# TensorE's order written out by hand in three attention stages

## The chip, the cores and the metric
The kernel runs on one core of a Trainium2 chip. The time is the device time of one launch in microseconds (us), the median of 3 runs. TensorE (PE) multiplies matrices and transposes, VectorE (DVE) and ScalarE (ACT) work on whole tiles, GpSimd (POOL) does a few copies, SyncE's queue (SP) starts the transfers from memory.

## What is computed
Two layers of a first block and one of a second, on 512 tokens of width 1024 in 32-bit floats. All three have an attention of 8 heads of width 64, and other projections of the same input beside it. Cut to this:

```
# first block, twice (l = 0, 1)
u = rmsnorm(x, norm_mix[l]);  proj = u @ w_in[l]
q, k, v, iq, ik, iw, cB, cC, ch, g = split(proj)          # q, k with rotary positions
s = q @ k.T / 8, kept where an index score is among the largest
y_attn = (softmax(s) @ v) @ w_attn_out[l]
gates = sigmoid(g)                                        # 2 x 1024 columns
x = x + (gates0 * y_attn + gates1 * y_conv) @ w_mix_out[l];  x = x + mlp(x)
# second block
qa, ka, va, qm, km, vm, og, ig, fg = split(h @ w_in)
attn = dilated attention of qa, ka, va                    # 3 patterns, added by their weights
qm, km = silu(short convolution of qm, km)
hm = chunked mLSTM(qm, km, vm, gates of ig, fg);  y = concat(attn, hm) @ w_out
```

## The kernel before
**Products in three matmuls.** A 32-bit factor is split into a high part, rounded to the type that the matmuls take (fp32r), and the low rest. A product is hi·hi + lo·hi + hi·lo. The weights are split as they come: `split` casts on ScalarE (L222) and subtracts on VectorE (L223), into rings of four buffers. So a cast of a weight unit waits until TensorE is done with the unit four before it.

**Projections.** `linear` makes a list of pieces. A piece is one column tile of 128 with 4 of the 8 blocks of the inner dimension: 4 x 3 = 12 matmuls of 512 columns, on L290, L291 and L292 (in `linear_tok`, used for the values of the mLSTM, L441 to L443, 6 matmuls a piece). The first piece of a weight unit carries a mark at which later units are fetched and split.

**Attention.** The 8 heads go in 4 pairs, the 512 queries in 4 blocks of 128. A unit is one pair and one block (`attn_unit`), 16 in a stage, and has three parts. `scores` (L555): two matmuls for each head, 128, 256, 384 or 512 keys wide (at least 256 on TensorE); VectorE adds the mask and reduces (L558), ScalarE takes the exponential (L563, with its sum), VectorE inverts that (L565), ScalarE scales (L566). `transp` (L574): one transpose for each block of 128 keys and head; the result is copied out of its bank by VectorE (L577) for head 0 and by ScalarE (L579) for head 1. `product`, once for a pair: 40 matmuls (L589) with the values into one bank, then a split on ScalarE and VectorE (L466, L467).
The score matmuls need their operands stacked: high and low part above each other (`two_part`, L605 and L606; `doubled`, L612 to L614, and a copy by GpSimd, L615). `parts` does both heads of a pair.

**Banks.** Four accumulation banks serve the projections (mm), three serve scores and transposes (at), one the products (ot). Within a unit the heads take one at bank each, and the bank goes on to the third tile behind it: head 1 of the transposes of a unit gets the bank that head 0 of the next unit's scores had.

**What sets the order.** `attn_pieces` gives a list: operands, the scores of unit t, the transposes of unit t - 1, and the product of a pair when its last unit is transposed. `interleave` mixes this list with the pieces of projections: the first gate (16 pieces, L894 to L897) in the first block, the convolution's and the mLSTM's projections in the second block (L1387 to L1394), where three functions of the gates, `gates1` to `gates3`, hang on pieces too. This list is not yet the order on an engine. A scheduler takes the list as priority and puts the instructions of each engine in an order by its own estimate of when their operands are there; so transposes, scores and products can be split up and mixed with projection matmuls.

Of the kernel before, what the change touches and what calls it, by code (L numbers as in the profile page):

```python
# [126 lines left out]
def blocks_kernel(ctx: ExitStack, tc: tile.TileContext, a: dict, out: bass.AP, stop=None):  # L127
# [114 lines left out]
    def linear(W, row0, kts, c0, widths, xs, evac, parts_=1, narrow=False, newbank=mmbank, bytile=False, skip=0):  # L242
# [23 lines left out]
        for part in range(parts_):  # L266
            cs = slice(part * TW, (part + 1) * TW)
            for kbase, kt, us in steps:
                for u in us:
# [3 lines left out]
                    for j, w in enumerate(widths):  # L273
# [5 lines left out]
                        def emit(u=u, j=j, o=o, w=w, kb=kbase, kt=kt, cs=slice(skip, T) if skip and w == P else cs):  # L279
                            if kb == 0:  # L280
                                bank[j] = newbank()
                            n = cs.stop - cs.start
                            ps = bank[j][:w, :n]
                            for k in range(kt):
                                hi, lo = xs(kb + k)
                                wh = u["hi"][:, k, o : o + w]
                                wl = u["lo"][:, k, o : o + w]
                                st = kb + k == 0
                                en = kb + k == total - 1
                                pe.matmul(ps, wh, hi[:, cs], start=st, stop=False)  # L290
                                pe.matmul(ps, wh, lo[:, cs], start=False, stop=False)  # L291
                                S["pe"] = pe.matmul(ps, wl, hi[:, cs], start=False, stop=en)  # L292
                            if kb + kt == total:
# [248 lines left out]
    def attn_unit(pair, i, stacks, PT, V, bias, O):  # L542
# [4 lines left out]
        def scores():  # L547
            qs, ks = stacks[pair]
            if i == NT - 1:
                stacks.pop(pair)  # L550
# [67 lines left out]
    def parts(q32, k32):  # L618

        qs, ks = [], []  # L620
        for hh in range(2):
            r = slice(64 * hh, 64 * hh + 64)
            o = slice(64 - 64 * hh, 128 - 64 * hh)
            qs.append(two_part(r, o, q32[r]))
            ks.append(doubled(r, o, k32[r]))
        return qs, ks

    def attn_pieces(q, k, V, bias, O):

        stacks = {}  # L630

        def stack(pair):
            def f():
                stacks[pair] = parts(q.pop(pair), k.pop(pair))
            return ("do", f)
# [4 lines left out]
        pieces = []  # L640
        I.append(stack(0))
        for t in range(n + 2):
            p = []
            if t < n and t % NT == 1 and t // NT < 3:
                p.append(stack(t // NT + 1))
            if t < n:
                p.append(("do", us[t][0]))
            if 1 <= t <= n:
                p.append(("do", us[t - 1][1]))
            if t >= 2 and t % NT == 1:  # L650
                p.append(("do", us[t - 2][2]))
            for it in p:
                pieces.append([it])
        return pieces
# [33 lines left out]
    def layer1(l, nextprep):  # L688
# [205 lines left out]
        for g in range(2):  # L894
            g0p += linear(W, 0, [4, 4], 3396 + 512 * g, [P] * 4, xs, evg0(g))
        at = attn_pieces(q, k, lambda j: V[j], bias, O)
        I.extend(interleave(at, g0p))  # L897
# [265 lines left out]
    def block2():  # L1163
# [223 lines left out]
        pieces = linear(W, 0, [4, 4], 1536, [P] * 4, xs, evconv(qm, 0))  # L1387
        pieces[2] = pieces[2] + [("do", gates1)]
        pieces[6] = pieces[6] + [("do", gates2)]
        pk = linear(W, 0, [4, 4], 2048, [P] * 4, xs, evconv(km, 4))  # L1390
        pk[4] = pk[4] + [("do", gates3)]
        pieces += pk
        pieces += linear_tok(W, 2560, xs, evv(vm))
        I.extend(interleave(attn_pieces(q, k, lambda j: V[j], db, O), pieces))  # L1394
# [384 lines left out]
```

## Time and profile before
| | |
|---|---|
| median of 3 runs | 2046.41 us (2046.17 to 2046.44) |
| the profiled execution | 2044.83 us, its span 2043.0 us |
| mean granted clock of TensorE | 0.997 of full speed |
| PE busy | 2026.1 us, 99% of the span |
| VectorE, ScalarE busy | 76%, 48% |
| stage 1, first score to the first matmul of `w_attn_out` | 223.22 to 299.48 us |
| stage 2, likewise | 921.31 to 997.58 us |
| stage 3, from the first projection of its own | 1486.56 to 1589.43 us |

The span is the time from the first to the last instruction in the trace. A stage is the stretch of one attention. A row of a timeline gives start and duration, the engine, the line and the operation, the tiles written and read, and the number of instructions; in brackets stands how long the engine stood idle before it and what released it. Matmuls are pipelined: the time from one start to the next is what a matmul takes from PE, the duration in the row is longer.

### The profile page before, as it was taken

Reading aid. Unit: us, or ns where it says so; the run is one execution under the profiler, and the core shown is the slowest. Engines: PE = TensorE matmul, PEld = TensorE weight load, DVE = VectorE, ACT = ScalarE, POOL = GpSimd, SP = SyncE. Lnnn points to the kernel's source line nnn. Section 1 sums busy time; section 2 is a strip of 40 time slices with the busy share of each in tenths; the row PEclk is TensorE's granted clock in tenths of the full one; section 3 lists DMA queues with packets and bytes.
Section 4 is the critical chain, followed back from the end, with each engine's and each line's share of the span. In section 5 each row is a group of like instructions: output and inputs, shape, how many; then the busy total and the mean of one; then the engine's idle time right before and its main releaser. Section 6 shows DMA issues by size and latency. Waiting matters only on the chain.

```text
span 2043.0 us, 29780 instructions
## 1 busy us (share of the span) xinstructions
PE 2026.1 (99%) x11632; PEld 1754.7 (86%) x11632; DVE 1547.0 (76%) x2783; ACT 986.6 (48%) x1713; POOL 19.5 (1%) x33
## 2 busy tenths in 40 slices
PE   9999999999999999999999999999999998999999
PEld 7888888899999888888888999999877797999998
DVE  6998667888787659977678888877777386777775
ACT  5323774644444432338655444455377754444442
POOL 0000000000000000000000000000010000000000
PEclk9999999999999999999999999999999999999999
DMA  7233223344444332331224444443221131332321
GB/s 248 83 94 102 73 63 93 100 149 149 150 155 147 105 105 83 100 96 63 73 93 134 145 155 134 155 134 88 87 83 54 50 114 32 104 103 94 114 94 42
DMA packets 203116, 216.62 MB, mean 106 GB/s; under 512 B 10720, under 2 KB 182112, under 8 KB 202976
## 3 DMA queue, kind: packets, MB, share of 16 engines
q1 hardware_dynamic: 202976, 214.73, 33.8%
q8 instruction: 91, 1.49, 0.3%
q14 instruction: 49, 0.40, 0.1%
HBM read 212.60 MB, written 2.10 MB: 105 GB/s over the span
## 4 chain that ended last, share of the span: by engine, by line
PE 95%; DVE 2%; ACT 1%; DMA 0%; issue 0%; SPq 0%; POOL 0%; DVEq 0%; ACTq 0%; POOLq 0%
PE mm L290 14%; PE mm L291 13%; PE mm L292 13%; PE mm L414 7%; PE mm L413 7%; PE mm L412 7%; PE at L290 7%; PE at L291 7%; PE at L292 7%; PE at L555 2%; PE mm L441 1%; PE mm L442 1%; PE mm L443 1%; PE ot L589 1%; PE at L574 1%; PE mm L1583 1%
## 5 line engine op out<-in xcount | busy, mean ns | idle before, releaser
L222 ACT CAST wh<-raw 128x1024 fp32r<-128x1024 f32 (+3 forms) x278 | 283.6, 1023 | 535.0 <-PE mm L413 221.6
L290 PE MATMUL mm<-g,wh 128*128 128x512 f32 (+2 forms) x1360 | 512.6, 378 | 1.7 <-ACT g L1103 1.6
L292 PE MATMUL mm<-g,wl 128*128 128x512 f32 (+2 forms) x1360 | 512.9, 377 | 0.0
L291 PE MATMUL mm<-g,wh 128*128 128x512 f32 (+2 forms) x1360 | 510.4, 375 | 0.0
L223 DVE TENSOR_TENSOR wl<-raw,wh 128x1024 fp32r<-128x1024 f32 (+3 forms) x278 | 329.3, 1186 | 141.3 <-ACT wh L222 140.3
L414 PE MATMUL mm<-g,wl 128*128 128x256 f32 x1288 | 364.6, 283 | 0.0
L413 PE MATMUL mm<-g,wh 128*128 128x256 f32 x1288 | 364.5, 283 | 0.0
L412 PE MATMUL mm<-g,wh 128*128 128x256 f32 x1288 | 363.9, 283 | 0.0
L290 PEld LDWEIGHTS mm<-g,wh 128*128 128x128 f32 x1360 | 255.8, 188 | 49.6 <-issue 4.3
L292 PEld LDWEIGHTS mm<-g,wl 128*128 128x128 f32 x1360 | 256.2, 188 | 45.5 <-issue 1.0
L291 PEld LDWEIGHTS mm<-g,wh 128*128 128x128 f32 x1360 | 256.1, 188 | 44.2 <-DVE g L475 0.3
L412 PEld LDWEIGHTS mm<-g,wh 128*128 128x128 f32 x1288 | 246.8, 192 | 4.7
L413 PEld LDWEIGHTS mm<-g,wh 128*128 128x128 f32 x1288 | 246.8, 192 | 4.6
L414 PEld LDWEIGHTS mm<-g,wl 128*128 128x128 f32 x1288 | 246.8, 192 | 0.2
L290 PE MATMUL at<-g,g 128*128 128x512 f32 x592 | 231.9, 392 | 0.0
L291 PE MATMUL at<-g,g 128*128 128x512 f32 x592 | 231.8, 392 | 0.0
L292 PE MATMUL at<-g,g 128*128 128x512 f32 x592 | 230.6, 389 | 0.1
L222 ACT CAST wh<-ws 128x1024 fp32r<-128x1024 f32 x69 | 72.3, 1048 | 182.3 <-PE mm L413 170.1
L292 PEld LDWEIGHTS at<-g,g 128*128 128x128 f32 x592 | 111.2, 188 | 24.7 <-DVE g L223 0.8
L223 DVE TENSOR_TENSOR wl<-ws,wh 128x1024 fp32r<-128x1024 f32 x69 | 84.5, 1224 | 59.7 <-ACT wh L222 59.7
L290 PEld LDWEIGHTS at<-g,g 128*128 128x128 f32 x592 | 111.7, 189 | 19.9
L291 PEld LDWEIGHTS at<-g,g 128*128 128x128 f32 x592 | 111.7, 189 | 18.6
(272 smaller groups left out, 2685.4 us busy)
## 6 DMA issues: line engine op xcount, KB each, us to landing
raw<-w_in SPq DMA_DIRECT2D x111, 512.0 KB, 3.8
raw<-w_mlp_up SPq DMA_DIRECT2D x64, 512.0 KB, 3.8
raw<-w_mlp_down SPq DMA_DIRECT2D x64, 512.0 KB, 3.6
g<-w_ada SPq DMA_DIRECT2D x96, 256.0 KB, 4.2
raw<-w_gate SPq DMA_DIRECT2D x22, 512.0 KB, 3.7
raw<-w_up SPq DMA_DIRECT2D x22, 512.0 KB, 3.6
raw<-w_down SPq DMA_DIRECT2D x22, 512.0 KB, 3.4
raw<-w_mix_out SPq DMA_DIRECT2D x16, 512.0 KB, 3.7
```

The source lines that it names most:

```text
L222: act.copy(hi, raw)
L223: dve.tensor_sub(lo, raw, hi.bitcast(F32))
L290: pe.matmul(ps, wh, hi[:, cs], start=st, stop=False)
L291: pe.matmul(ps, wh, lo[:, cs], start=False, stop=False)
L292: S["pe"] = pe.matmul(ps, wl, hi[:, cs], start=False, stop=en)
L412: pe.matmul(ps, wh, hi, start=first and m == 0 and k == 0, stop=False, skip_group_check=True)
L413: pe.matmul(ps, wh, lo, start=False, stop=False, skip_group_check=True)
L414: S["pe"] = pe.matmul(ps, wl, hi, start=False, stop=k == 3, skip_group_check=True)
L441: pe.matmul(ps, xh, wh, start=kb + k == 0, stop=False)
L442: pe.matmul(ps, xl, wh, start=False, stop=False)
L443: pe.matmul(ps, xh, wl, start=False, stop=kb + k == KT - 1)
L555: pe.matmul(ps[:, :WM], qs[hh][:, i * P : (i + 1) * P], ks[hh][n][:, :WM], start=n == 0, stop=n == 1)
```

## The change
A new function `attention` takes the place of `attn_pieces` and of `interleave`. In it TensorE's instructions stay in the order in which they are written, from the first scores to the last product (`tc.manual_schedule` with TensorE as its one engine); the other engines are ordered by the scheduler as before. The order is a list of steps: the scores of a unit; the transposes of the unit before, with the operands of one head of the next pair (head 0 at the second unit of a pair, head 1 at the third), and with the product of the pair before where it is due. Behind each step stands its share of the other projections. With `fine=True` their pieces of 12 matmuls are cut into two of 6. The last product stands behind all of them. Both heads' operands of the first pair stand ahead of the first step.

```diff
-    def linear(W, ..., bytile=False, skip=0):
+    def linear(W, ..., bytile=False, skip=0, fine=False):
...
-                            if kb == 0:
+                            if kb + ks[0] == 0:
                                 bank[j] = newbank()
...
-                            for k in range(kt):
+                            for k in ks:
...
-                        pieces.append(([("unit", u)] if first else []) + [("do", emit)])
-                        first = False
+                        for ks in (range(0, kt // 2), range(kt // 2, kt)) if fine else (range(kt),):
+                            pieces.append(([("unit", u)] if first else []) + [("do", lambda emit=emit, ks=ks: emit(ks))])
+                            first = False
...
-    def attn_pieces(q, k, V, bias, O):
+    def attention(q, k, V, bias, O, others):
+        def stack(pair, hh):
             def f():
-                stacks[pair] = parts(q.pop(pair), k.pop(pair))
-            return ("do", f)
+                r = slice(64 * hh, 64 * hh + 64)
+                o = slice(64 - 64 * hh, 128 - 64 * hh)
+                q32, k32 = (q[pair], k[pair]) if hh == 0 else (q.pop(pair), k.pop(pair))
+                stacks[pair, hh] = two_part(r, o, q32[r]), doubled(r, o, k32[r])
+            return f
+        def enter():
+            region["r"] = tc.manual_schedule(engines={nc.tensor.engine})
+            region["r"].__enter__()
...
-        I.append(stack(0))
+        do(stack(0, 0))
+        do(stack(0, 1))
+        do(enter)
+        steps = [[]]
         for t in range(n + 2):
-            p = []
-            if t < n and t % NT == 1 and t // NT < 3:
-                p.append(stack(t // NT + 1))
             if t < n:
-                p.append(("do", us[t][0]))
+                steps.append([us[t][0]])
             if 1 <= t <= n:
-                p.append(("do", us[t - 1][1]))
+                steps.append([us[t - 1][1]])
+                if t % NT in (1, 2) and t // NT < 3:
+                    steps[-1].append(stack(t // NT + 1, t % NT - 1))
             if t >= 2 and t % NT == 1:
-                p.append(("do", us[t - 2][2]))
-            for it in p:
-                pieces.append([it])
-        return pieces
+                steps[-1].append(us[t - 2][2])
+        done = 0
+        last = steps[-1].pop()
+        for m, st in enumerate(steps):
+            for f in st:
+                do(f)
+            upto = (m + 1) * len(others) // len(steps)
+            add(others[done:upto])
+            done = upto
+        do(last)
+        do(leave)
...
-        pieces = linear(W, 0, [4, 4], 1536, [P] * 4, xs, evconv(qm, 0))
-        pieces[2] = pieces[2] + [("do", gates1)]
+        pieces = linear(W, 0, [4, 4], 1536, [P] * 4, xs, evconv(qm, 0), fine=True)
+        pieces[4] = pieces[4] + [("do", gates1)]
```

`gates2` and `gates3` move from pieces 6 and 4 to half pieces 12 and 8 of their lists in the same way. In the first block the 16 pieces of the first gate are cut in halves and handed to `attention`.

What stands in a row on the engines, in three places. The lines of the kernel after lie 2 further in `attn_unit` (scores L557, reduction L560, transposes L576, copies L579 and L581, product L591, operands L607 to L617), and 15 or 16 further from the first block's code on. The numbers behind a tile's name tell tiles apart and differ between the kernels.

TensorE at the start of the third stage, before. Thirteen projection matmuls of this stage stand ahead of these rows; at tiles are banks of scores:
```order
L291 MATMUL mm_14349<-g_13358,wh_14173 128x512
L555 MATMUL at_14268<-g_14253,g_14250 128x256
L292 MATMUL mm_14349<-g_13357,wl_14174 128x512
L290 MATMUL mm_14349<-g_13363,wh_14173 128x512
L291 MATMUL mm_14349<-g_13364,wh_14173 128x512
L555 MATMUL at_14268<-g_14254,g_14250 128x256
L292 MATMUL mm_14349<-g_13363,wl_14174 128x512
L290 MATMUL mm_14349<-g_13369,wh_14173 128x512
L291 MATMUL mm_14349<-g_13370,wh_14173 128x512
L555 MATMUL at_14279<-g_14262,g_14259 128x256
L555 MATMUL at_14327<-g_14253,g_14250 128x256
L555 MATMUL at_14327<-g_14254,g_14250 128x256
```

The same place after, with three projection matmuls of the stage ahead of these rows:
```order
L290 MATMUL mm_14282<-g_13369,wh_14179 128x512
L291 MATMUL mm_14282<-g_13370,wh_14179 128x512
L292 MATMUL mm_14282<-g_13369,wl_14180 128x512
L557 MATMUL at_14289<-g_14259,g_14256 128x256
L557 MATMUL at_14289<-g_14260,g_14256 128x256
L557 MATMUL at_14300<-g_14268,g_14265 128x256
L557 MATMUL at_14300<-g_14269,g_14265 128x256
L290 MATMUL mm_14282<-g_13375,wh_14179 128x512
L291 MATMUL mm_14282<-g_13376,wh_14179 128x512
L292 MATMUL mm_14282<-g_13375,wl_14180 128x512
```

The first score matmul moved from behind 14 matmuls of the stage to behind 6, and the two heads of the first unit are no longer taken apart.

VectorE in the first pair of the first stage, before, from the copy of the transposes of unit 1 (L577) to the next inversions (ISA on L558 is the reduction of a head, its second row the read of its sum; the mask is bias):
```order
L577 COPY g_2031<-at_2028 128x256
L565 RECIPROCAL rec_2001<-den_1999 128x1
L565 RECIPROCAL rec_2012<-den_2010 128x1
L558 ISA g_2041,nm_2042<-at_2038,bias_1194 128x512
L558 ISA nm_2042 128x1
L558 ISA g_2052,nm_2053<-at_2049,bias_1194 128x512
L558 ISA nm_2053 128x1
L577 COPY g_2064<-at_2060 128x384
L565 RECIPROCAL rec_2046<-den_2044 128x1
L565 RECIPROCAL rec_2057<-den_2055 128x1
```

The same place after. L608 and L616 are the subtractions of the next pair's operands for head 1, L223 is that of a weight unit:
```order
L579 COPY g_2024<-at_2021 128x256
L223 TENSOR_TENSOR wl_2145<-raw_1845,wh_2144 128x1024
L567 RECIPROCAL rec_2001<-den_1999 128x1
L567 RECIPROCAL rec_2012<-den_2010 128x1
L608 TENSOR_TENSOR g_2031<-g_818,g_2031 64x512
L616 TENSOR_TENSOR g_2035<-g_1001,g_2034 64x512
L560 ISA g_2056,nm_2057<-at_2053,bias_1194 128x512
L560 ISA nm_2057 128x1
L560 ISA g_2067,nm_2068<-at_2064,bias_1194 128x512
L560 ISA nm_2068 128x1
L579 COPY g_2085<-at_2081 128x384
L567 RECIPROCAL rec_2061<-den_2059 128x1
```

A weight subtraction and two operand subtractions now stand between the copy of unit 1 and the reductions of the 512-wide scores (L560); before, the operands of the next pair were done at one stretch between units 0 and 1 and the weight's behind unit 1's reductions.

VectorE in the third stage, before, at the end of the gates' scans (L1362 adds what L1357 scanned, L467 subtracts for a split):
```order
L1362 TENSOR_TENSOR g_14851<-g_14851,g_14853 128x512
L223 TENSOR_TENSOR wl_15023<-raw_14750,wh_15022 128x1024
L467 TENSOR_TENSOR g_14866<-g_14853,g_14865 128x512
L558 ISA g_14872,nm_14873<-at_14869,g_13505 128x512
L558 ISA nm_14873 128x1
L558 ISA g_14883,nm_14884<-at_14880,g_13505 128x512
```

The same place after, with the scans (L1372) and the scores of the unit behind them:
```order
L223 TENSOR_TENSOR wl_15033<-raw_14717,wh_15032 128x1024
L1372 SCALAR_TENSOR_TENSOR g_14918<-g_14909 128x128
L1376 TENSOR_TENSOR mst_14920<-g_14918,g_14916 128x1
L1372 SCALAR_TENSOR_TENSOR g_14918<-g_14909,mst_14920 128x128
L1376 TENSOR_TENSOR mst_14923<-g_14918,g_14916 128x1
L1372 SCALAR_TENSOR_TENSOR g_14918<-g_14909,mst_14923 128x128
L1376 TENSOR_TENSOR mst_14926<-g_14918,g_14916 128x1
L1372 SCALAR_TENSOR_TENSOR g_14918<-g_14909,mst_14926 128x128
L1377 TENSOR_TENSOR g_14916<-g_14916,g_14918 128x512
L468 TENSOR_TENSOR g_14931<-g_14918,g_14930 128x512
L560 ISA g_14950,nm_14951<-at_14947,g_13511 128x256
L560 ISA nm_14951 128x1
```

The scans, with their sum and the subtraction of L468, stand in one block ahead of the reductions of 256-wide scores, which is unit 9; before they stood ahead of the 512-wide ones of unit 7, with the convolution's operations (L1377) among the scans.

## Rows read from the trace of the kernel before
**Rows 1.** the page: busy time of each engine, and the last chain by engine.
```profile
PE 2026.1 (99%) x11632; PEld 1754.7 (86%) x11632; DVE 1547.0 (76%) x2783; ACT 986.6 (48%) x1713; POOL 19.5 (1%) x33
...
PE 95%; DVE 2%; ACT 1%; DMA 0%; issue 0%; SPq 0%; POOL 0%; DVEq 0%; ACTq 0%; POOLq 0%
```
**Rows 2.** PE's waits: line <- releaser: us in total, times, longest.
```profile
PE at L574 <- DVE nm L558: 2.0, 3, 0.9
```
**Rows 3.** timeline, start of stage 3: start, duration us, engine, line.
```profile
1486.56 0.39 PE L290 MATMUL mm<-g,wh 128*128 128x512 f32 x1
...
1489.84 0.38 PE L555 MATMUL at<-g,g 128*128 128x256 f32 x1
...
1490.47 1.15 POOL L615 CAST g<-g 64x512 fp32r<-64x512 f32 x1 [120.56 <-DVE g L614]
...
1491.67 0.39 PE L555 MATMUL at<-g,g 128*128 128x256 f32 x1 [0.75 <-POOL g L615]
...
1492.30 0.61 POOL L615 CAST g<-g 64x512 fp32r<-64x512 f32 x1 [0.68 <-DVE g L614]
```
**Rows 4.** timeline of PE, projection matmuls, the first and the thirteenth.
```profile
1496.65 0.39 PE L291 MATMUL mm<-g,wh 128*128 128x512 f32 x1
...
1499.37 0.39 PE L291 MATMUL mm<-g,wh 128*128 128x512 f32 x1
```
**Rows 5.** timeline of PE, a broken product and a whole one.
```profile
261.83 1.74 PE L589 MATMUL ot<-g,g 128*64 128x128 f32 x26
264.46 0.30 PE L574 MATMUL at<-kon,g 128*128 128x128 f32 x1 [0.89 <-DVE nm L558]
264.69 1.09 PE L589 MATMUL ot<-g,g 128*64 128x128 f32 x14
...
282.06 1.20 PE L589 MATMUL ot<-g,g 128*64 128x128 f32 x18
```
**Rows 6.** two stretches: busy us (instructions) of each engine, PEclk, DMA.
```profile
223.00:298.00 75.00, 74.08 (x493) 61.01 (x491) 50.23 (x143) 64.20 (x148) 4.11 (x6) 1.00 0.19 57
...
1415.00:1420.00 5.00, 5.00 (x28) 4.88 (x28) 2.39 (x8) 0.62 (x2) 0.00 (x0) 0.66 0.00 0
```
**Rows 7.** timeline of stage 3, VectorE's scans and PE's transposes behind them.
```profile
1539.16 0.48 DVE L1357 TENSOR_TENSOR_SCAN g<-g,mst 128x128 f32<-128x128 f32 x1
...
1541.10 0.69 DVE L1362 TENSOR_TENSOR g<-g,g 128x512 f32<-128x512 f32 x1
...
1544.05 0.08 DVE L558 DVE_READ_ACCUMULATOR2_ANT nm<- 128x1 f32 x1
...
1544.19 0.55 PE L574 MATMUL at<-kon,g 128*128 128x128 f32 x3 [0.20 <-DVE nm L558]
...
1544.49 0.48 PE L291 MATMUL mm<-g,wh 128*128 128x512 f32 x1
```
**Rows 8.** timeline of PE, a wait outside the attention stages.
```profile
1414.37 0.74 PE L290 MATMUL mm<-g,wh 128*128 128x256 f32 x4 [1.62 <-ACT g L1103]
```
**Rows 9.** groups of stage 1: xcount | busy us, mean ns | idle before.
```profile
L222 ACT CAST wh<-raw 128x1024 fp32r<-128x1024 f32 x8 | 8.4, 1049 | 5.4 <-PE mm L291 5.3
...
L223 DVE TENSOR_TENSOR wl<-raw,wh 128x1024 fp32r<-128x1024 f32 x8 | 9.7, 1218 | 0.6 <-ACT wh L222 0.6
...
L613 ACT CAST g<-g 64x512 fp32r<-64x512 f32 x6 | 3.7, 618 | 0.1
...
L614 DVE TENSOR_TENSOR g<-g,g 64x512 fp32r<-64x512 f32 x6 | 4.4, 736 | 1.1 <-ACT g L612 1.0
...
L558 DVE CUSTOM_DVE_ANT_0 g<-at,bias 128x512 f32<-128x512 f32 x8 | 5.3, 688 | 0.8 <-PE at L555 0.8
...
L579 ACT COPY g<-at 128x256 f32<-128x256 f32 x4 | 1.4, 351 | 0.0
```
**Rows 10.** timeline, start of stage 1.
```profile
223.22 0.88 PE L555 MATMUL at<-g,g 128*128 128x256 f32 x6
...
224.78 1.28 ACT L563 ACT_TABLE_LOAD   x1
```

More of the change, by code (lines that the diff above doesn't have):

```diff
@@ L240, in halves, with linear @@
         return us
-    def linear(W, row0, kts, c0, widths, xs, evac, parts_=1, narrow=False, newbank=mmbank, bytile=False, skip=0):
+    def linear(W, row0, kts, c0, widths, xs, evac, parts_=1, narrow=False, newbank=mmbank, bytile=False, skip=0, fine=False):
         pieces = []
@@ L277, in linear, with emit @@
                             continue
-                        def emit(u=u, j=j, o=o, w=w, kb=kbase, kt=kt, cs=slice(skip, T) if skip and w == P else cs):
-                            if kb == 0:
+                        def emit(ks, u=u, j=j, o=o, w=w, kb=kbase, kt=kt, cs=slice(skip, T) if skip and w == P else cs):
+                            if kb + ks[0] == 0:
                                 bank[j] = newbank()
@@ L547, in scores @@
         def scores():
-            qs, ks = stacks[pair]
+            qs, ks = zip(*(stacks[pair, hh] for hh in range(2)))
             if i == NT - 1:
-                stacks.pop(pair)
+                for hh in range(2):
+                    stacks.pop((pair, hh))
             WM = max(W, 2 * P)
@@ L616, in doubled, with leave @@
         return kh, kl
[L618 to L626, printed above, removed]
-    def attn_pieces(q, k, V, bias, O):
+    def attention(q, k, V, bias, O, others):
         stacks = {}
-        def stack(pair):
+        region = {}
+        def stack(pair, hh):
             def f():
-                stacks[pair] = parts(q.pop(pair), k.pop(pair))
-            return ("do", f)
+                r = slice(64 * hh, 64 * hh + 64)
[6 more added lines that the diff above has]
+            region["r"].__enter__()
+        def leave():
+            region.pop("r").__exit__(None, None, None)
         PT = {}
@@ L894, in layer1 @@
         for g in range(2):
-            g0p += linear(W, 0, [4, 4], 3396 + 512 * g, [P] * 4, xs, evg0(g))
-        at = attn_pieces(q, k, lambda j: V[j], bias, O)
-        I.extend(interleave(at, g0p))
+            g0p += linear(W, 0, [4, 4], 3396 + 512 * g, [P] * 4, xs, evg0(g), fine=True)
+        attention(q, k, lambda j: V[j], bias, O, g0p)
         def sig0():
@@ L1386, in block2 @@
         db = lambda i: C2["db"][:, (3 - i) * P : T]
-        pieces = linear(W, 0, [4, 4], 1536, [P] * 4, xs, evconv(qm, 0))
-        pieces[2] = pieces[2] + [("do", gates1)]
-        pieces[6] = pieces[6] + [("do", gates2)]
-        pk = linear(W, 0, [4, 4], 2048, [P] * 4, xs, evconv(km, 4))
-        pk[4] = pk[4] + [("do", gates3)]
+        pieces = linear(W, 0, [4, 4], 1536, [P] * 4, xs, evconv(qm, 0), fine=True)
+        pieces[4] = pieces[4] + [("do", gates1)]
+        pieces[12] = pieces[12] + [("do", gates2)]
+        pk = linear(W, 0, [4, 4], 2048, [P] * 4, xs, evconv(km, 4), fine=True)
+        pk[8] = pk[8] + [("do", gates3)]
         pieces += pk
         pieces += linear_tok(W, 2560, xs, evv(vm))
-        I.extend(interleave(attn_pieces(q, k, lambda j: V[j], db, O), pieces))
+        attention(q, k, lambda j: V[j], db, O, pieces)
         def post_attn():
```

3 lines of the change are left out of this document (1 added, 2 removed).

## The prediction
> **What bounds the kernel now.** I read the page first: PE is busy 99% of the span, and the chain of work that ended last is 95% PE [rows 1]. So a change pays only where PE now stands still or spends more time than its matmuls need, and it costs wherever PE is made to wait. Then the table of PE's waits: beside waits in other parts of the program it has 2.0 us in three waits of transposes (L574) for VectorE's score reductions (L558) [rows 2], all in the attention stages, and the start of the third stage adds 0.75 us in a score matmul (L555) that waits for GpSimd's copy [rows 3]. Little is left to win there. Third, PE's timeline in the stages, for what an order costs that shows as no wait. A projection matmul follows the one before in 0.227 us (twelve steps from 1496.65 to 1499.37) [rows 4]. A product in one run of 40 matmuls is busy for 2.40 us. One that a transpose breaks takes 1.74 for 26 matmuls and 1.09 for the other 14, with the lone transpose between, 0.23 from start to start (264.46 to 264.69) [rows 5]. Last, the queues of ScalarE and VectorE, because the new PE order forces PE to follow them: in the first stage ScalarE is busy 64.20 of 75 us and VectorE 50.23 [rows 6].
>
> **What the change can win.** (S_t and T_t are the scores and the transposes of unit t, one pair of heads and one block of 128 queries, numbered 0 to 15 in a stage.) The broken product costs 1.74 + 1.09 - 2.40 = 0.43, and its lone transpose takes 0.23 where three in a group take 0.30 from start to the next start (1544.19 to 1544.49, [rows 7]), about 0.10 each, so 0.55 a break. The orders show two breaks in each of the first two stages and six in the third: 10 x 0.55 = 5.5 us, all on PE and so all on the path. If the four waits of the attention stages go as well, 2.0 + 0.75 = 2.7 us more. Together 8.2 us. The half pieces, each of 6 x 0.227 = 1.37 us, are the same matmuls in the same number. Switches between kinds of work become fewer (27 groups of transposes become 16 in each stage); no row prices one apart from a break, so I take nothing for them and leave up to 0.1 each, 33 x 0.1 = 3 us, for the lower end.
>
> **What the change adds: waits at the start of the third stage.** Before, 14 projection matmuls stand ahead of the first score matmul, and 3, 3 more between the next ones. PE starts at 1486.56, the first score issues at 1489.84 and the second at 1491.67, when GpSimd's first copy (1490.47, 1.15 us) is done; the second copy runs 1492.30 to 1492.91 [rows 3]. In the changed order 6 matmuls stand ahead, so PE is at the first score at 1486.56 + 1.37 = 1487.93, and all four scores follow with nothing between. The operand casts on ScalarE, VectorE and GpSimd keep their order here, so the operands come no sooner: PE stands 1.9 us until 1489.84, 1.7 until 1491.67, then about 1.1 until the second copy is done, since a written order lets nothing pass. That is 4.7 us, against bounds of 0.75 (the operands could be ready before 1489.84, and the row only shows PE's turn) and 5.0 (1487.93 to 1492.91). The eight matmuls that stood there before are done later, and hide nothing new.
>
> [...]
> [...]
>
> **Waits inside the steps, first and second stage.** The three score banks turn over so that the head-1 transposes of unit t take the bank of the head-0 scores of unit t+1, and wait until VectorE has reduced those. In the written order PE does 6 matmuls, 1.37 us, between the two, and nothing more to fall back on. On VectorE the subtractions of the next pair's operands now stand ahead of these reductions, where before all stood in one block behind the first unit. For T_2 of the first pair I laid the queues side by side from the stage's first score at 223.22 [rows 10]. At the end of a weight cast (L222) PE has just done T_1. From there ScalarE has two exps, a bank copy, a cast, two scalings and a cast, seven instructions of 0.35 to 0.62 (from start to start), about 3.5 us, until the operand is there that VectorE's second subtraction waits for; then 0.65 for it and 0.61 for the 512-wide reduction, and 0.14 until PE moves (as from 1544.05 to 1544.19, [rows 7]): 4.9 us [rows 9]. PE from the same moment has 6 matmuls, the 512-wide scores (4 x 0.23, as wide as a projection matmul), 6 matmuls and three transposes, 1.37 + 0.92 + 1.37 + 0.30 = 4.0. The wait is 0.9, say 1.0. For T_6, in the second pair, a weight subtraction (1.22) takes the place of a cast there: 1.2 us. T_0 waits about 0.45, for the table load (1.28, [rows 10]) and a third exp now stand ahead of the first scaling; T_10 about 0.2. This is 2.85 a stage, 5.7 for two, between 0 (VectorE catches up while PE waits elsewhere) and 8.7 (the other three of the six units with operand casts ahead of their reductions wait 0.5 each, in both stages).
>
> **Waits inside the steps, third stage.** The scans of the gates stand ahead of S_9's reductions. Three scan periods take 1.94 us (1539.16 to 1541.10); four, the sum behind them (0.69) and a subtraction of the same size come to 3.9 us, and before, with 25 projection matmuls between, the transposes still waited 0.20 [rows 7]. Now there are 12 matmuls and a score group, 3.2 us, before T_8's head 1. The wait is between 0.2 and, if the weight subtraction that stands ahead of the scans (1.22, [rows 9]) and the reduction (0.35, as half of 0.69) come on top, 3.9 + 1.2 + 0.35 - 3.2 = 2.3; I take 1.5, since of such a block all but 0.20 was hidden before. T_10, with three casts, a weight cast and its subtraction ahead of the reduction, has the same ends and I take 1.5 for it too.
>
> **The sum.** 4.7 + 1.7 + 5.7 + 3.0 = 15.1 us of new waits, less 8.2 won, is +6.9 us. The profiled execution took 2044.83 (span 2043.0), the median of the runs is 2046.41, so 2051.7 in such an execution and 2053.3 as a median; I say 2053.
>
> **Rivals.** One: the steps have no waits at all. The mechanism is that VectorE, whose reductions release most banks, is idle a third of the stage (50.23 busy of 75) and that PE's wait at each stage's start lets it get ahead by more than the 1.0 to 1.5 us that the T groups lack; from there the 8.2 and up to 3 of the switches are kept, the start costs 4.7 less the 8 matmuls of slack that it may still find, no clock fall. Then 2046.4 - 8.2 - 2 + 4.7 = 2041, faster. Against it: ScalarE, which feeds VectorE's subtractions, is busy 86% of the stage, so it doesn't get ahead. Two: waits about half as long as I sum them (4.3 in the steps, 4.7 at the start, no fall): +0.8, so 2047. For it: each wait delays PE, and so spares the next. [...] Four: the change doesn't do what it says, PE's order being nearly what it was. The orders speak against it (14 matmuls ahead of the first score become 6), so I give it nothing of its own.
>
> **How the numbers follow.** Forecast 0.47, three 0.15, two 0.25, one 0.13. A measurement of this kernel can tell 0.2% from no change, 4.1 us: faster is below 2042.3, slower above 2050.5. Of the forecast's own range, 2049 to 2058, a sixth lies below 2050.5. So slower 0.39 + 0.15 + some of rival two's upper end 0.05 = 0.59, faster 0.11, same 0.30. The range runs from rival one's upper half, 2042, to past rival three, 2061.
>
> **What would show it.** At the third stage's start a PE wait of near 4.7 us at the score line, the larger part named GpSimd's copy, and a granted clock of about 0.7 in the 5 us behind it. In PE's table of waits the transposes' wait for the reductions at 5 to 9 us instead of 2.0, with T_2 and T_6 in it in both of the first stages. Each of the 12 products in one run, busy for 2.40 us. Wrong would be: no such rows and a shorter third stage, or a wait that falls on another engine, such as weight casts that arrive late because the matmuls that free their buffers now come later.

## The result: 0.65% slower, and the profile after

The changed kernel takes 2059.06 us (2057.47 to 2059.9, 4 runs), the one before 2046.29 us beside it. The ratio is 1.0065, with a 95% interval of 1.0053 to 1.0077; the two medians alone give 1.0062, or 12.8 us. The forecast was 2053, in a range of 2042 to 2061, and slower. So the sign and the mechanism hold, but the loss is 12.8 us where 6.9 were summed. The profiled execution took 2059.9 us, the longest of the four, with a span of 2057.8.

The page of the kernel after, the busy times and the engines' shares of the last chain [rows 1]:
```profile
PE 2028.8 (99%) x11632; PEld 1761.7 (86%) x11632; DVE 1546.7 (75%) x2783; ACT 987.4 (48%) x1713; POOL 19.2 (1%) x33
...
PE 93%; ACT 3%; DVE 2%; issue 1%; DMA 0%; POOL 0%; SPq 0%; DVEq 0%; ACTq 0%; POOLq 0%
```
PE's share of the chain fell from 95% to 93%, which points to stretches in which PE waits; the size can't be read from it, because two points of share are some 40 us. TensorE's work itself did not grow: the same 11632 matmuls, busy 2.7 us longer. The slow clock below adds more than that to its busy time (6.8 us), and the breaks that are gone take some of it off again.

The table of PE's waits after, in us in total, times, longest; L576 is the transposes, L557 the scores, L560 VectorE's reduction, L615 a cast on ScalarE, L617 GpSimd's copy [rows 2]:
```profile
PE at L576 <- DVE nm L560: 11.2, 8, 2.4
...
PE at L557 <- POOL g L617: 1.9, 2, 1.4
...
PE at L557 <- ACT g L615: 1.8, 1, 1.8
```
The transposes wait 11.2 us for reductions where it was 2.0, and the first scores of the third stage 3.7 where it was 0.75.

The start of the third stage after, start and duration in us [rows 3]:
```profile
1490.22 0.39 PE L290 MATMUL mm<-g,wh 128*128 128x512 f32 x1
...
1493.49 0.39 PE L557 MATMUL at<-g,g 128*128 128x256 f32 x1 [1.75 <-ACT g L615]
...
1494.13 1.14 POOL L617 CAST g<-g 64x512 fp32r<-64x512 f32 x1 [119.02 <-DVE g L616]
...
1495.33 0.80 PE L557 MATMUL at<-g,g 128*128 128x256 f32 x2 [1.45 <-POOL g L617]
...
1495.95 0.61 POOL L617 CAST g<-g 64x512 fp32r<-64x512 f32 x1 [0.68 <-PE at L557]
...
1496.62 0.58 PE L557 MATMUL at<-g,g 128*128 128x256 f32 x1 [0.49 <-POOL g L617]
```
The first projection of the stage starts at 1490.22, six follow one another until 1491.58, and there PE stands until the operands are there: first for a cast of ScalarE (L615), then twice for GpSimd's copies. The operands come no sooner than before: the first copy starts 3.91 us behind the stage's first projection in both kernels (1490.47 after 1486.56, 1494.13 after 1490.22). From start to start PE loses 1.91, 1.72 and 1.04 us, 4.7 in all as summed; the table above shows 3.7, because it counts idle time from the modelled end of a matmul, and so has 1.75, 1.45 and 0.49 here, less by 0.16, 0.27 and 0.55.

T_2 of the first pair in the first stage, with what stands ahead of its bank on ScalarE and VectorE (L222 weight cast, L614 operand cast, L616 operand subtraction, L560 the 512-wide reduction):
```profile
233.05 1.05 ACT L222 CAST wh<-raw 128x1024 fp32r<-128x1024 f32 x1 [0.55 <-PE mm L291]
...
233.30 0.38 PE L576 MATMUL at<-kon,g 128*128 128x128 f32 x2
...
237.18 0.49 PE L576 MATMUL at<-kon,g 128*128 128x128 f32 x3
...
237.37 0.61 ACT L614 CAST g<-g 64x512 fp32r<-64x512 f32 x1
...
238.01 0.69 DVE L616 TENSOR_TENSOR g<-g,g 64x512 fp32r<-64x512 f32 x1 [1.10 <-ACT g L614]
...
238.73 0.69 DVE L560 CUSTOM_DVE_ANT_0 g<-at,bias 128x512 f32<-128x512 f32 x1
...
239.57 0.52 PE L576 MATMUL at<-kon,g 128*128 128x128 f32 x3 [1.90 <-DVE nm L560]
```
PE does the three transposes of head 0 at 237.18 and could go on at 237.5. Head 1 needs the bank of the 512-wide scores, whose reduction starts at 238.73 because the operand subtraction stands ahead of it, and that waits for a cast that ends at 238.0. PE goes on at 239.57.

T_8 in the third stage, behind the gates' scans (L1372) and their subtraction (L468) [rows 7]:
```profile
1549.68 0.43 DVE L1372 TENSOR_TENSOR_SCAN g<-g 128x128 f32<-128x128 f32 x1 [0.91 <-ACT g L1365]
...
1553.06 0.69 DVE L468 TENSOR_TENSOR g<-g,g 128x512 fp32r<-128x512 f32 x1
...
1553.67 0.42 DVE L560 CUSTOM_DVE_ANT_0 g<-at,g 128x256 f32<-128x256 f32 x1
...
1554.15 0.33 PE L576 MATMUL at<-kon,g 128*128 128x128 f32 x1 [1.33 <-DVE nm L560]
```
The scans begin at 1549.68, the reduction of the 256-wide scores at 1553.67; T_8's head 1 waits 1.33 us.

T_10, with a weight cast (L222) and its subtraction (L223) ahead of the reduction:
```profile
1567.04 1.05 ACT L222 CAST wh<-raw 128x1024 fp32r<-128x1024 f32 x1
...
1568.12 1.22 DVE L223 TENSOR_TENSOR wl<-raw,wh 128x1024 fp32r<-128x1024 f32 x1
...
1569.26 0.68 DVE L560 CUSTOM_DVE_ANT_0 g<-at,g 128x512 f32<-128x512 f32 x1
...
1570.10 0.75 PE L576 MATMUL at<-kon,g 128*128 128x128 f32 x3 [2.43 <-DVE nm L560]
```
The weight subtraction of 1.22 us at 1568.12 and the reduction behind it hold T_10's head 1 back by 2.43 us.

T_5, behind the subtraction of a product's split (L468):
```profile
1534.40 0.68 DVE L468 TENSOR_TENSOR g<-ot,g 128x512 fp32r<-128x512 f32 x1
...
1535.00 0.54 DVE L560 CUSTOM_DVE_ANT_0 g<-at,g 128x384 f32<-128x384 f32 x1
...
1535.60 0.44 PE L576 MATMUL at<-kon,g 128*128 128x128 f32 x2 [1.73 <-DVE nm L560]
```
Here VectorE works without a pause from the operands' first subtraction at 1531.75 on; T_5's head 1 waits 1.73 us.

The granted clock at and behind five of the waits, in stretches of 5 us (busy us and instructions of each engine, then the clock) [rows 6]:
```profile
239.00:244.00 5.00, 4.42 (x28) 3.90 (x28) 2.81 (x14) 4.54 (x14) 0.45 (x1) 1.00 0.01 2
935.00:940.00 5.00, 3.09 (x15) 2.50 (x14) 3.23 (x8) 4.08 (x10) 0.61 (x1) 0.88 0.35 105
940.00:945.00 5.00, 5.00 (x25) 4.17 (x25) 1.54 (x8) 3.90 (x11) 0.00 (x0) 0.78 0.00 0
1495.00:1500.00 5.00, 4.18 (x12) 3.31 (x13) 1.50 (x6) 2.80 (x7) 0.88 (x2) 0.52 0.10 40
1500.00:1505.00 5.00, 5.00 (x21) 4.16 (x21) 1.55 (x9) 3.49 (x10) 0.00 (x0) 0.80 0.00 0
1535.00:1540.00 5.00, 4.40 (x21) 3.67 (x22) 3.76 (x11) 4.32 (x10) 0.00 (x0) 1.00 0.22 54
1569.00:1574.00 5.00, 3.90 (x14) 3.35 (x15) 4.29 (x12) 3.76 (x8) 0.82 (x1) 0.66 0.31 105
```
A drop of the granted clock to 0.50 of full speed is called a fall below. The second stage's, in stretches of 1 us:
```profile
938.00:939.00 1.00, 0.33 (x2) 0.36 (x3) 1.00 (x3) 0.45 (x1) 0.53 (x1) 0.89 0.00 0
939.00:940.00 1.00, 1.00 (x5) 0.90 (x4) 0.67 (x4) 1.00 (x5) 0.00 (x0) 0.50 0.00 0
940.00:941.00 1.00, 1.00 (x4) 0.71 (x4) 0.16 (x1) 1.00 (x3) 0.00 (x0) 0.50 0.00 0
941.00:942.00 1.00, 1.00 (x4) 0.81 (x3) 0.00 (x0) 0.66 (x2) 0.00 (x0) 0.50 0.00 0
942.00:943.00 1.00, 1.00 (x8) 0.91 (x7) 0.53 (x4) 0.24 (x1) 0.00 (x0) 0.90 0.00 0
943.00:944.00 1.00, 1.00 (x7) 0.79 (x6) 0.33 (x2) 1.00 (x6) 0.00 (x0) 1.00 0.00 0
```
After T_2's wait in the first stage (1.90 us) the clock stayed up. After the same wait of 1.91 in the second stage it is 0.88 and 0.78 in two stretches. The start of the third stage cost 0.52 and 0.80 in two stretches, T_5's wait of 1.73 at 1535.60 nothing, and T_10's 0.66. In the third stage such stretches read 0.50 from 1496 to 1501 and from 1571 to 1573, and projection matmuls start 0.43 us apart there (1497.42 to 1497.85), against 0.227 [rows 4]. By the shares the three stretches with a fall hold 3.4, 6.8 and 3.4 us at 0.50, and PE lost half of that: 1.7, 3.4 and 1.7 us.

The last product of the first stage and the matmul behind it [rows 5]:
```profile
299.95 2.40 PE L591 MATMUL ot<-g,g 128*64 128x128 f32 x40
302.29 0.50 PE L290 MATMUL mm<-g,wh 128*128 128x512 f32 x1
```
It runs in one piece, busy 2.40 us, as all 12 now do.

The stages, each from its first score (the third from its first projection) to the first matmul behind it, in us; idle time is what the trace shows within it:

| stage | before | after | more | idle before, after | lost to the clock |
|---|---|---|---|---|---|
| 1 | 76.26 | 77.22 | 1.0 | 0.9, 2.9 | 0 |
| 2 | 76.27 | 78.82 | 2.6 | 0.9, 2.9 | 1.7 |
| 3 | 102.87 | 113.08 | 10.2 | 1.0, 9.5 | 5.1 |

Together 13.7 us. In the first stage 2.0 us of waits are added and 1.0 more is won elsewhere; 2 breaks at 0.55 are 1.1. In the third, 8.5 of waits and 5.1 of clock less 6 x 0.55 come to 10.3. The rest of the difference between the two profiles, 1.0 us, lies outside the stages: the first projection matmuls of the program came 0.43 us apart up to 10.4 us, in the profile before some 0.23 apart from 6.25 us on (1.9 us more at the first stage's first score, 225.07 against 223.22), the fall of the clock near 1415 us in the profile before [rows 6, 8] did not occur (1.7 less between the second stage and the third), and 0.9 us more lies behind the third stage and was not taken apart. The first two differ among the kernels below as well: the fall near 1415 us is there in four of their ten profiles.

### The profile page after: what moved, and what is told of

Its sections match the earlier page's. It is cut to its first block, busy times and chain, and to the rows that moved or that the text cites. A ratio compares the mean times of both kernels' runs of the same rounds, so it can differ in the third digit from the quotient of the medians.

```text
span 2057.8 us, 29772 instructions
## 1 busy us (share of the span) xinstructions
PE 2028.8 (99%) x11632; PEld 1761.7 (86%) x11632; DVE 1546.7 (75%) x2783; ACT 987.4 (48%) x1713; POOL 19.2 (1%) x33
## 4 chain that ended last, share of the span: by engine, by line
PE 93%; ACT 3%; DVE 2%; issue 1%; DMA 0%; POOL 0%; SPq 0%; DVEq 0%; ACTq 0%; POOLq 0%
PE mm L290 13%; PE mm L291 13%; PE mm L292 13%; PE mm L415 8%; PE mm L414 7%; PE mm L413 7%; PE at L290 7%; PE at L291 7%; PE at L292 7%; PE mm L442 1%; PE mm L443 1%; PE mm L444 1%; PE ot L591 1%; PE at L576 1%; PE at L557 1%; PE mm L1598 1%
## 5 line engine op out<-in xcount | busy, mean ns | idle before, releaser
L222 ACT CAST wh<-raw 128x1024 fp32r<-128x1024 f32 (+3 forms) x278 | 283.8, 1022 | 535.1 <-PE mm L414 221.5
L223 DVE TENSOR_TENSOR wl<-raw,wh 128x1024 fp32r<-128x1024 f32 (+3 forms) x278 | 329.1, 1185 | 141.6 <-ACT wh L222 140.6
L222 ACT CAST wh<-ws 128x1024 fp32r<-128x1024 f32 x69 | 72.3, 1048 | 183.0 <-PE mm L414 170.8
L223 DVE TENSOR_TENSOR wl<-ws,wh 128x1024 fp32r<-128x1024 f32 x69 | 84.4, 1224 | 59.7 <-ACT wh L222 59.7
```

Of the source, the lines that this page charges most:

```text
L222: act.copy(hi, raw)
L223: dve.tensor_sub(lo, raw, hi.bitcast(F32))
```

## The experiments

All times are medians, and each ratio is to runs of the kernel before on the same chip, which took 2045.0 to 2045.5 there and spread over 2043.4 to 2048.8. The changed kernel was not run beside them, so whatever is compared with it goes by two ratios, each with an interval of about 0.0012 to either side, some 2.5 us. The first theory: the change loses by waits of PE that its fixed order lets nothing fill, and by the clock that falls behind them.

**More work ahead of the third stage.**
```diff
+        add(others[:lead])                # lead = 5 in the third stage, 0 in the others
+        others = others[lead:]
         done = 0
```


> The third stage begins with five half pieces (30 projection matmuls) ahead of its first step; the rest of the order of the changed kernel stays. Theory (the loss is PE's waits plus the falls of its clock behind them): the 3.7 us of waits at the first scores go to under 0.5, and with them the fall of the clock there (3.4 us of lost work), so about 7 us less than the changed kernel, near 2052. Rival (the waits only move: the five half pieces are missing later, and the steps that lose them wait for VectorE as long): 2057 or more, with the transposes' waits for the reductions up from 5.7 us in this stage to 9 or more.


2055.73 us, ratio 1.0055 (1.0043 to 1.0068), 2 us better than the change by the ratios, whose intervals overlap; its profiled execution is the slowest of five (2058.44). Its waits:
```profile
PE at L576 <- DVE nm L560: 11.4, 9, 2.5
...
PE at L557 <- DVE g L579: 2.0, 1, 2.0
...
PE at L557 <- ACT g L1367: 0.7, 1, 0.7
```
The waits for GpSimd's copy at the start are gone, as the theory had it, but the stage's idle time fell only from 9.5 to 8.6 us: a score group at 1520.62 now waits 2.0 us for VectorE's copy (L579), and another 0.7 for a copy of the gates (L1367). The rival is right in kind: with a fixed order, projections that are spent at the start are missing between later steps. Its signs were too high, though: the time is under 2057, and the transposes' waits in this stage are 5.9 us where 9 or more were named.

**Four banks in turn.** Head 1 of a unit's transposes gets the bank of the transposes of the unit before, or that of a product that stood between.
```diff
+    def abank():
+        turn[0] += 1
+        return otbank() if turn[0] % 4 == 0 else atbank()
-                ps = atbank()      # scores, transposes
+                ps = abank()
-            ops = otbank()         # product
+            ops = abank()
```


> Scores, transposes and products of the attention take turns in four banks instead of three and one, so that head 1 of a unit's transposes no longer gets the bank of the next unit's head-0 scores; TensorE's order stays as in the changed kernel. Theory (the steps wait because of that bank): the transposes' waits for reductions fall from 11.2 us to under 2, two falls of the clock of 1.7 each go with them, 13 us less, near 2046, with 3.7 us still at the third stage's start. Rival (VectorE and ScalarE are late in any case, the bank is only the first to show it): the waits take another name, the scaling on ScalarE or the bank of a product, and the time is 2055 or more.


2051.96 us, ratio 1.0036 (1.0022 to 1.005): about 6 us better than the change by the ratios, less than half of what the theory gave. The profile is of the fastest of five executions (2048.66, 11 us under the change's), with a mean granted clock of 0.996 where the other four have 0.994 to 0.995, so the others had, by estimate, more falls than it shows. In the first two stages the theory holds: 0.5 us of idle time each instead of 2.9, and no fall of the clock (1.00 in both). In the third stage 7.5 of 9.5 us stay:
```profile
PE at L563 <- POOL g L623: 1.9, 2, 1.4
...
PE at L563 <- DVE nm L566: 1.7, 2, 0.9
...
PE ot L597 <- DVE nm L566: 1.2, 1, 1.2
...
PE at L582 <- DVE g L474: 1.0, 1, 1.0
```
3.7 are the start as it was, and the other 3.8 have new names: scores that wait for a bank still being reduced, a product behind another reduction, and transposes behind the subtraction of a product's split (L474). There the rival holds in kind: in the third stage VectorE is late, whatever the bank. Its bound of 2055 was not reached.

**Both together**, the two edits above:
```diff
+        add(others[:lead])                # lead = 5 in the third stage
+        others = others[lead:]
...
-                ps = atbank()
+                ps = abank()
...
-            ops = otbank()
+            ops = abank()
```


> Both edits, the five half pieces ahead of the third stage and the four banks in turn. Theory: the waits and falls of both go, 2059 - 7 - 13 = 2039, below the kernel before by the 5.5 us of its ten broken products and some 2 us of its waits. Rival: the written order costs PE something beside its waits, and the time stays at or above 2046.


2047.84 us, ratio 1.0013 (1.0005 to 1.0022). The theory's 2039 is missed and the rival's bound of 2046 met, but not for its reason: the clock is 1.00 throughout the third stage, and 6.2 us of waits remain in it, among them a product that stands 1.9 us for a reduction:
```profile
PE ot L597 <- DVE nm L566: 1.9, 1, 1.9
```
What the written order costs there is still waits; the edits had moved part of them.

**The scheduler orders TensorE, the list stays.**
```diff
-        do(enter)
...
-        do(leave)
```


> The list of steps, the half pieces and the operands head by head stay, but TensorE's order is left to the scheduler again. Theory (the written order on TensorE is what makes it wait): PE's waits are as few as before, under 3 us in the attention stages; seven products or so are still broken; near the kernel before, 2044 to 2048. Rival (the half pieces and the operands head by head put VectorE's work in the wrong order, whoever orders TensorE): waits of 8 us or more, 2052 or more.


2042.58 us, ratio 0.9988 (0.9979 to 0.9996), faster than the kernel before. Its waits:
```profile
PE at L576 <- DVE nm L560: 1.6, 5, 0.3
...
PE at L557 <- POOL g L617: 0.8, 1, 0.8
```
1.6 us of waits in five instead of 11.2 in eight, and the third stage takes 100.9 us from its first projection (1484.07) to the first matmul behind it (1584.96), where the kernel before has 102.9 and the change 113.1. Ten breaks have become six, two in each stage. Taken together, the half pieces, the operands head by head and the steps are sound; keeping TensorE to the list is what cost some 16 us (0.9988 against 1.0065).

**The written order in two stages only.**
```diff
-        do(enter)
+        if written:                # written = False in the third stage
+            do(enter)
...
-        do(leave)
+        if written:
+            do(leave)
```


> TensorE's order is written out in the first two stages only; in the third the scheduler orders it, from the same list. Theory (the cost of the written order lies where VectorE and ScalarE have other work to do, in the third stage): the first two stages cost what they cost in the changed kernel, 2 x 2.0 us of waits more than before, 2.2 less for four whole products, one fall of the clock of 1.7, and the third is 1.6 shorter than before: about 2 us over the kernel before. Rival (each stage pays alike for the written order): 8 us over it.


2047.18 us, ratio 1.0008 (1.0 to 1.0017), some 2 us over the kernel before (2044.99) in an interval that reaches down to no difference: as the theory had it, and far from the rival's 8. In its profile the clock fell behind T_2's wait in both of the first stages (each 78.6 us to the last product's matmuls, where the change had 77.0 and 78.6), so which of these waits brings a fall changes from one execution to another.

**The operands of both heads in one step**, ahead of the scores of a pair's second unit instead of behind two groups of transposes.
```diff
             if t < n:
                 steps.append([us[t][0]])
+                if t % NT == 1 and t // NT < 3:
+                    steps[-1][:0] = [stack(t // NT + 1, 0), stack(t // NT + 1, 1)]
             if 1 <= t <= n:
                 steps.append([us[t - 1][1]])
-                if t % NT in (1, 2) and t // NT < 3:
-                    steps[-1].append(stack(t // NT + 1, t % NT - 1))
```


> The changed kernel, but with the operands of both heads of the next pair in one step, ahead of the scores of a pair's second unit, as in the kernel before. Theory (T_2 waits because operand subtractions stand ahead of its reduction on VectorE): the waits of T_2 (1.90 in each of the first two stages) fall under 0.3, the fall of the clock behind one of them goes, and in the third stage the waits of T_5 and T_10 (1.73, 2.43) shrink by half at least: 6 to 8 us less than the changed kernel. Rival (ScalarE and VectorE have as much to do in any order, so the same wait shows up one or two units earlier): within 2 us of the changed kernel.


2083.76 us, ratio 1.0188 (1.0174 to 1.0202), by far the slowest and missed by both. Its waits, and T_0 of the first stage:
```profile
PE at L576 <- DVE nm L560: 28.1, 9, 7.3
```
```profile
227.19 0.60 ACT L614 CAST g<-g 64x512 fp32r<-64x512 f32 x1
...
229.60 0.62 ACT L615 CAST g<-g 64x512 fp32r<-64x512 f32 x1
...
229.81 0.69 DVE L616 TENSOR_TENSOR g<-g,g 64x512 fp32r<-64x512 f32 x1
...
230.53 0.42 DVE L560 CUSTOM_DVE_ANT_0 g<-at,bias 128x256 f32<-128x256 f32 x1
...
231.11 0.45 PE L576 MATMUL at<-kon,g 128*128 128x128 f32 x1 [3.78 <-DVE nm L560]
```
T_2 and T_5 wait no more, and T_10's wait falls to 1.13, as the theory had it. But the block of six casts now stands ahead of S_1's reduction: the last subtraction (L616) starts at 229.81, the reduction at 230.53, and T_0's head 1 waits 3.78 us. The same block makes T_4 and T_8 wait, 2.0 us each in the first two stages, 4.1 and 7.3 in the third. So the rival saw the place, but not the size: with both heads at one place the waits are 28.1 us instead of 11.2, and no fixed price for a block follows, since one and the same block costs 2.0 or 3.8. The mean clock of the run falls to 0.989. This also prices the operands head by head: under a written order they save 25 us (1.0188 against 1.0065).

**Four banks, and the scheduler orders TensorE.**
```diff
-        do(enter)
...
-                ps = atbank()
+                ps = abank()
-            ops = otbank()
+            ops = abank()
```


> The scheduler orders TensorE, from the list of steps with half pieces, and scores, transposes and products take turns in four banks. Theory (a product is broken because transposes wait for a bank, so the fourth bank mends both waits and breaks): all 12 products in one run, no wait over 0.5 us in the steps, 2.7 us better than the kernel before as without the banks, and 7 breaks of 0.43 more: 5.5 to 6 us under it. Rival (where the scheduler is free it hides the bank's wait anyway): 2 to 3 us under it.


2037.31 us, ratio 0.9961 (0.9948 to 0.9973): 8 us under the kernel before, the fastest of all, and 2 us better than the theory, although one wait (0.6) is over the theory's 0.5. What is left of the waits in the stages:
```profile
PE at L563 <- POOL g L623: 0.7, 1, 0.7
...
PE ot L597 <- DVE nm L566: 0.6, 1, 0.6
...
PE at L563 <- DVE nm L566: 0.2, 1, 0.2
```
1.5 us. The scheduler, where a transpose's bank is free, breaks no product at all, where it broke six with three banks; in the kernel before with four banks (the next run) there are 3 breaks instead of 10. So most of those breaks were its way around the bank.

**The kernel before with four banks.**
```diff
-                ps = atbank()
+                ps = abank()      # in the kernel before, nothing else
-            ops = otbank()
+            ops = abank()
```


> The kernel before with the four banks in turn and nothing else. Three products are broken instead of ten. Theory (breaks at 0.55 us each and the bank's waits are what the attention stages lose): 7 x 0.55 + 1.5 = 5 us under the kernel before. Rival (the half pieces are what makes the scheduler's order better): within 1 us of it.


2041.23 us, ratio 0.9981 (0.9972 to 0.999), 3.8 us less with 3 breaks instead of 10 (the ten were in seven products, not ten as expected above). Between the two theories, nearer to the first: 7 x 0.55 alone is 3.9, and the waits in the stages stayed at 2.8 to 2.9 us.

**No operand casts behind the first pair.** The scores of the pairs 1 to 3 use the first pair's operands; the kernel leaves the others out, so that its result is not the attention's.
```diff
-            if i == NT - 1:
+            if i == NT - 1 and pair > 0:
...
+                if pair == 0:
                     stacks[pair, hh] = two_part(r, o, q32[r]), doubled(r, o, k32[r])
+                else:
+                    stacks[pair, hh] = stacks[0, hh]
```


> The changed kernel without the operand casts of the second to fourth pair in each stage: their scores use the first pair's operands, so 18 casts on ScalarE, 12 subtractions on VectorE and 6 copies on GpSimd a stage are left out. TensorE's work and order stay. Theory (T_2, T_5, T_6 and T_10 wait because these stand ahead of the reductions): of 11.2 us of waits of transposes for reductions those of T_2, T_6, T_5 and T_10 go (2 x 2.7 + 1.73 + 2.43 = 9.6), T_8's 1.3 behind the gates' scans stays, and the falls of the clock behind them go: 10 to 13 us under the changed kernel, 2047 to 2049. Rival (six matmuls are too little for the reduction itself, casts or not): waits of 6 us or more stay.


2045.74 us, ratio 1.0002 (0.9993 to 1.0011), 13 us under the change.
```profile
PE at L576 <- DVE nm L560: 2.7, 3, 1.3
```
Of 11.2 us 2.7 stay: T_8's 1.27 behind the scans, as expected, 1.13 of T_10, which still has the weight subtraction ahead of its reduction, and 0.34 of T_5. T_2 and T_6 no longer wait, and the first two stages have 0.18 us of idle time each. So six matmuls between scores and transposes are enough for the reduction itself. What made it late were the casts and subtractions queued ahead of it. That this is their place and not only their amount is shown by the run with the operands of both heads in one step, where the same casts at another place end the waits of T_2 and T_5 and bring others.

**Four banks, the written order in two stages only.**
```diff
-        do(enter)
+        if written:                # written = False in the third stage
+            do(enter)
...
-        do(leave)
+        if written:
+            do(leave)
...
-                ps = atbank()
+                ps = abank()
...
-            ops = otbank()
+            ops = abank()
```


> Four banks in turn; TensorE's order written out in the first two stages and left to the scheduler in the third. With four banks the scheduler's own order differs from the written one in the first pair of a stage only. Theory (a written order costs only what it makes TensorE wait): within 1.5 us of the kernel with four banks and the scheduler throughout, that is 6 to 8 us under the kernel before. Rival (a written order costs something beside waits): 3 us or more above that one.


2040.74 us, ratio 0.9974 (0.9964 to 0.9985), 2.7 us above the scheduler throughout, between the bounds of the two theories, with intervals that overlap. The first two stages are 1.2 us longer each than there (74.8 against 73.6 to the last product), of which 0.35 is idle time more. Counted from start to start, in the first stage, T_0 loses 0.5 us and the scores near 237 us 0.8, where the scheduler's order has nothing and 0.4 at the same places, so some 0.9 of the 1.2 are waits; the rest was not taken apart.

## Why the prediction was right, and what it mis-sized

- **The start of the third stage** was right to the step: 4.7 us from start to start, the first part released by ScalarE's cast and the larger rest (2.8) by GpSimd's two copies. That the eight projections moved behind it hide nothing new was right as well.
- **Waits in the first two stages**: 2.85 us each was forecast, 2.92 measured, but not unit by unit. T_2 took 1.90 instead of 1.0, because the weight cast ahead of the operand casts itself waited for TensorE and ended some 0.5 us behind T_1 instead of with it, and because ScalarE's seven instructions behind it took 3.9 us instead of 3.5; T_6 took 0.84 instead of 1.2, T_0 0.18 instead of 0.45, T_10 nothing. The errors cancel: that the total fits is luck. The cause, operand subtractions ahead of the reduction whose bank is needed, is shown by the run without casts (both waits go) and the one with the operands at another place (both go, and others come there).
- **Waits in the third stage**: 3.0 forecast, 5.7 measured. T_8 was 1.33 for 1.5. T_10 was 2.43, a little over its upper end of 2.3, and T_5 (1.73) was missing from the list: there the operands' two subtractions, two of the convolution's operations and the product's subtraction stand in a row on VectorE ahead of the reduction. Without the operand casts 0.34 of it stays.
- **The clock** is the term that was mis-sized most: 1.7 us in the sum, 6.8 in the profile (1.7 in the second stage, 3.4 at the third's start, 1.7 behind T_10). No run shows the sum's 1.7 as the price of the two gaps at the third stage's start; 3.4 us were lost there. What the kernel before shows is 1.7 lost by the fall behind the wait of 1.62 us near 1415 (a clock of 0.66 over 5 us, [rows 6, 8]); that fall is itself no rule: with the same wait it is there in five of the twelve profiles. With 2.7 more of waits in the third stage this makes 7.8 of difference, and explains a sum of 14.7 where the stages show 13.7. Rival three, with its 0.15 of the chances, stands for falls behind the waits of the steps too, and was right in kind: of the four waits of the steps between 1.7 and 2.5 us two brought a fall (T_2 in the second stage, T_10), and those of 1.33 and 0.84 brought none. The measured 2059 lies above the forecast's own 2049 to 2058 and inside the range only because the range was drawn past this rival.
- **What was won**: the ten breaks are gone, at about the price given (1.0 us in the first stage, 3.8 us for seven of them in the kernel before with four banks). The third stage had 29 groups of transposes before, not 27; nothing rests on it.
- **The first rival** (VectorE gets ahead) is refuted in the changed kernel, and what would make it true in the first two stages is shown: no operand casts ahead of the reductions. The second (half the waits, no fall) is refuted by 15.3 us of waits in the stages and three places with a fall, the fourth by the whole products.
- Not settled: which of several waits of the same length brings the clock down, the 0.9 us behind the third stage, and the last 0.3 us a stage between the written and the scheduler's order with four banks.

## What to carry to other kernels

An order written out by hand for the bounding engine is only as good as the queues of the engines that feed it: look up, for every step, which instruction frees its bank and what stands ahead of that one on its engine, and add the durations of the whole block. Where a scheduler broke up a run of matmuls, ask first which buffer it was avoiding; here the fourth bank in turn took 7 of 10 breaks from the kernel before (0.9981) and all that were left under the new list (0.9988 to 0.9961), while forbidding the breaks turned them into waits (1.0065). Price a wait on TensorE with the clock that may follow it: a fall cost 1.7 us here, and came behind six of the twelve waits near 2 us in the stages.

## What the runs showed of the hardware

The same wait of 1.90 us at the same place in two equal stages was followed by a fall of the granted clock in one and none in the other, and in another run by a fall in both. Over all profiles, the stages have twelve waits of 1.89 to 2.02 us; a fall followed six of them. The wait of 1.62 us outside the stages [rows 8] stands in all twelve profiles; a fall followed in five (the kernel before, more work ahead, four banks, and the two with the written order in two stages) and none in seven. In the changed kernel and in the one with more work ahead, the stretch behind it:
```profile
1420.00:1425.00 5.00, 5.00 (x41) 4.84 (x40) 3.92 (x12) 2.10 (x6) 0.00 (x0) 1.00 0.00 0
```
```profile
1420.00:1425.00 5.00, 5.00 (x32) 4.95 (x32) 2.40 (x8) 0.98 (x3) 0.00 (x0) 0.72 0.00 0
```
A single fall held some 3.4 us at 0.50 of full speed, a double one at the third stage's start 6.8. Such falls go with the spread of the times. The four runs of the changed kernel spread over 2.4 us and the kernel before beside it over 0.4, but in 21 other runs the kernel before spread over 5.4, from 2043.4 us at a mean granted clock of 0.998 to 2048.8 at 0.996; a difference of 0.002 is some 4 us of its span by estimate.
